# The expert layers' up-projection with coefficients as the stationary operand, and part of VectorE's splitting and one-hot work on GpSimd

## The chip, the cores and the metric

The kernel runs on one core of one Trainium2 chip, in one launch. The metric is the device time in microseconds (us). The kernel before has been run three times: 2917.88 us in the median, 2916.68 to 2918.5 us. TensorE (PE) multiplies matrices: one operand, 128 x 128 here, is loaded into the array and stays (the stationary operand, a weight load), the other is streamed through it column by column (the moving operand), and the products are added up in PSUM, the accumulators' memory. VectorE (DVE), ScalarE (ACT) and GpSimd (POOL) work elementwise, and SyncE (SP) starts the transfers. SBUF is the on-chip memory of 128 partitions.

## The reference, cut to what matters

256 tokens of width 1024 run through two layers of a first block (a mixer and an expert layer each) and two layers of a second block (a mixer, cross attention and a gated feed-forward layer each). The change touches the two expert layers alone:

```python
PEER_HEADS, PEER_NKEYS, PEER_TOPK = 8, 128, 16      # 128 * 128 = 16384 experts

def peer_ffn(x, w_query, sub_keys, down, up):
    q = (xt @ w_query).reshape(T, H, 2, PEER_HALF)
    s = jnp.einsum('thcd,cnd->thcn', q, sub_keys)
    sv, si = lax.top_k(s, K)                          # per half of the key
    ...                                               # the 16 best pairs i * 128 + j per head
    idx = jnp.take_along_axis(cand_i, pos, axis=-1)
    gate = jax.nn.softmax(top_s, axis=-1)
    ...
        a = jnp.einsum('thkd,td->thk', down[ib], xb)
        c = gb * jax.nn.gelu(a)
        return jnp.einsum('thk,thkd->td', c, up[ib])
```

Each token uses 8 x 16 = 128 of the 16384 experts.

## The kernel before

**No gather.** The kernel computes all 16384 experts for all 256 tokens and zeroes what a token did not choose. An expert's number is i * 128 + j. A *row* here is one i: 128 experts, a 128 x 1024 tile of `down` and one of `up`, 512 KB each. `dscan(half, dst)` multiplies 64 rows of `down` with the normalized tokens and writes gelu of the result to `ga[half]`, for each row 128 experts x 256 tokens. `build(half, dst)` makes, token by token, the matrix of gates and multiplies `ga` by it; what then lies in `ga` are the coefficients. `uscan(half)` multiplies 64 rows of `up` with the coefficients and adds up all 128 rows in four PSUM banks.

**The split.** For accuracy in fp32r each factor is cut into a high part h and a low part l, and a product is three matmuls, h*h, l*h and h*l (`mm3`, lines 303 to 305). A weight tile comes by DMA into `wr`, `wt` (line 248) casts it on ScalarE to `wh` (L255) and subtracts on VectorE, `wl = wr - wh` (L256). `wr`, `wh` and `wl` have four buffers each. The coefficients are split for two rows at a time by `split` (L293 on ScalarE, L294 on VectorE) into a ring of eight slots, `xh` and `xl`.

**The up-projection.** `row` (line 514) takes each of the eight 128 x 128 pieces of a row of `up` as the stationary operand and streams the coefficients, 256 tokens, as the moving one: 8 x 3 = 24 matmuls of 256 columns for a row. The result stands as width x tokens, as the residual `x` does. `tail` (line 410) computes the last two rows accumulator by accumulator and adds each to `x` at once (L425), so that the next stage's first matmuls find their input while the last are running.

**Build.** For a block of 8 tokens VectorE makes two one-hot matrices, `oj` (128 x 1024, fp16) and `oi` (128 x 512), by comparing with a ramp (both L1314), and `gi`, the products of `oi` with the two halves of the gates (L1329, 128 x 1024 fp16). TensorE multiplies them (L1338, 16 matmuls of 64 columns), and VectorE multiplies the result in PSUM into `ga` (L1320). There are two sets of `oj`, `oi` and `gi`. A build has 32 blocks; there are two builds a layer. `oj`, `gi` and `oi` appear in the rows as `sq` and `xres`, the tiles in whose room they lie.

**What sets the order.** `wt` calls `tick`, which runs side work (a generator) as long as it has credit: each weight tile adds R1 = 1150 (routing), R2 = 1500 (the first build, beside the second half of `dscan`) or R3 = 1600 (the second build, beside the first half of `uscan`), and a block costs 600 + 900 + 600 = 2100. With H1 = H2 = 0 side work on VectorE stands behind the last split issued. The rest of the order is a list scheduler's; engines run their own queue in order.

Of the kernel before, what the change touches and what calls it, by code (L numbers as in the profile page):

```python
# [23 lines left out]
F32 = mybir.dt.float32  # L24
# [5 lines left out]
OP = mybir.AluOpType  # L30
# [5 lines left out]
T = 256  # L36
# [161 lines left out]
class K:  # L198
    def __init__(self, ctx, tc, ap, ahead):
        self.tc, self.nc, self.ap, self.ctx = tc, tc.nc, ap, ctx  # L200
        nc = self.nc
        self.P = ctx.enter_context(tc.tile_pool(name="keep", bufs=1))
        self.W = ctx.enter_context(tc.tile_pool(name="wts", bufs=1))
        self.S = ctx.enter_context(tc.tile_pool(name="scr", bufs=1))
        self.ps = ctx.enter_context(tc.tile_pool(name="psum", bufs=1, space=PSUM))
        self.dr = ctx.enter_context(tc.tile_pool(name="dram", bufs=1, space=DRAM))
        self.x = self.P.tile([128, 8, T], F32, name="xres", bufs=1)
        self.nw = self.P.tile([128, 13, 8], F32, name="nw")
        self.eps = self.P.tile([128, 1], F32, name="eps")
        nc.vector.memset(self.eps, EPS)  # L210
        nc.scalar.copy(self.eps, self.eps)
        self.got = []
        for d in range(4):
            nc.sync.dma_start(self.x[:, 2 * d:2 * d + 2], ap["x"][:, 2 * d:2 * d + 2])
            if d == 0:
                nc.sync.dma_start(self.nw, ap["nw"])
                for w in ahead[:1]:
                    self.fetch(w)
        for w in ahead[1:]:
            self.fetch(w)  # L220
        self.ones = self.P.tile([128, 128], F32, name="ones")
        nc.vector.memset(self.ones, 1.0)
        self.ident = self.P.tile([128, 128], F32, name="ident")
        self.tb = None
        ps = self.pst("mx")[:, :128]
        for _ in range(WARM):
            nc.tensor.matmul(ps, self.ones, self.ones, start=True, stop=True)
        self.side, self.rate, self.credit = None, 0.0, 0.0
        self.lows, self.hold = [], None
        self.todo, self.sqs = [], []  # L230

    def cap(self, name, rows=128):
        o, w = _COFF[name]
# [14 lines left out]
    def wt(self, src, w=1024):  # L248
        nc = self.nc
        if not self.got:  # L250
            self.fetch(src)
        r = self.got.pop(0)
        h = self.W.tile([128, 1024], F32R, name="wh", bufs=4)
        l = self.W.tile([128, 1024], F32R, name="wl", bufs=4)
        nc.scalar.copy(h[:, :w], r[:, :w])  # L255
        self.lows.append(nc.vector.tensor_sub(l[:, :w], r[:, :w], h[:, :w].bitcast(F32)).ins.name)  # L256
        n = len(nc.cur_bb.bb.instructions)
        self.tick()
        if self.hold is not None and len(self.lows) > self.hold:
            for i in nc.cur_bb.bb.instructions[n:]:  # L260
                if i.engine == mybir.EngineType.DVE:
                    self.tc.add_manual_dep(i, self.lows[-1 - self.hold], mybir.DependencyInfo(
                        mybir.DependencyClass.NoSync, mybir.DependencyReason.DATA), reason="order")
        return h, l
# [145 lines left out]
    def tail(self, accs, rows, wi, scale=None):  # L410
# [27 lines left out]
        ps, rt, r = self.norm_room()  # L438
# [4 lines left out]
        self.rsqrt(rt, ps)  # L443
        self.diag(r, rt)
        self.bcast(r)

    def rows(self, accs, srcs, bhs, bls, end):

# [663 lines left out]
GS = 32768.0  # L1112
# [5 lines left out]
def peer(k, l, nxt):  # L1118
# [4 lines left out]
    with k.tc.tile_pool(name=f"peer_{l}", bufs=1) as p:  # L1123
# [168 lines left out]
                    V.tensor_sub(g3[:, :, 1], gb, g3[:, :, 0])  # L1292

        k.beside(routing(), R1, H1)
        dscan(0, ga[0])

        sets = [[room[:, starts[i]:starts[i + 1]] for i in range(3)],
# [4 lines left out]
        def build(half, dst):  # L1302
# [20 lines left out]
            for b in range(n + 1):  # L1323
                if b < n:
                    oj, oi, gi, ts_ = parts(b)
                    hot(oj, jS[:, ts_], slice(0, 128))
                    yield 600
                    hot(oi, iS[:, ts_], hs)
                    V.tensor_mul(gi.rearrange("p t q (a d) -> p t q a d", d=2),  # L1329
                                 oi.rearrange("p t (a d) -> p t a d", d=2)[:, :, None].to_broadcast([128, TB, 2, HI // 2, 2]),  # L1330
                                 g3[:, ts_, :, None].to_broadcast([128, TB, 2, HI // 2, 2]))
                    yield 900
# [10 lines left out]
        k.beside(build(0, ga[0]), R2, H2)  # L1343
        dscan(1, ga[1])
        k.drain()
        accs = k.rows_begin()
        ring = [k.S.tile([128, 8, T], F32R, name=n, bufs=1) for n in ("xh", "xl")]
        end = []

# [8 lines left out]
        def uscan(half):  # L1358
            for i in range(half * HI, (half + 1) * HI, 2):
                if i % HI == 0:  # L1360
                    coef(i)
                if i % HI + 2 < HI:
                    coef(i + 2)
                if i == 2 * HI - 2:
                    k.tail(accs, [k.wt(ap[f"up{l}"][e]) + tuple(at(e)) for e in (i, i + 1)], nxt, scale=1.0 / GS)
                else:
                    for e in (i, i + 1):
                        k.row(accs, *k.wt(ap[f"up{l}"][e]), *at(e), e == 0, False)

        k.beside(build(1, ga[1]), R3, H2)  # L1370
        uscan(0)
# [4 lines left out]
        k.x = k.P.tile([128, 8, T], F32, name="xres", bufs=1)  # L1376
        nc.sync.dma_start(k.x, xd)
        uscan(1)
        top.close()
    k.dbg("xp", k.x, l)  # L1380

# [383 lines left out]
```

## Time and profile before

| | |
|---|---|
| median of three runs | 2917.88 us (2916.68 to 2918.5) |
| the profiled execution | 2919.18 us, its span 2917.1 us |
| TensorE busy | 2889.8 us, 99% of the span, 25130 matmuls |
| weight loads | 2836.1 us, 97% |
| VectorE busy | 2077.0 us, 71% |
| ScalarE busy | 1457.7 us, 50% |
| GpSimd busy | 0.2 us, 4 instructions |
| DMA | 511.5 MB, 175 GB/s in the mean |

Busy time counts overlapping instructions once. A duration includes the time in which an instruction's last results leave the pipe, so on TensorE and VectorE the next one starts before the row's duration is over; what an instruction costs its engine in a dense stretch is the distance from its start to the next one's start. The layers of the first expert stage lie from about 230 to 1012 us, those of the second from about 1230 to 2010 us.

### The profile page before, as it was taken

What the parts mean: (1) busy time and instruction counts of PE and PEld (TensorE: products, weight loads), DVE (VectorE), ACT (ScalarE), POOL (GpSimd) and SP (SyncE); (2) the same over time, 40 slices, a digit from 0 to 9 for tenths busy, and PEclk for the clock granted to TensorE, in tenths of its full rate; (3) what the DMA queues carried; (4) which work ended last, traced back from release to release, by engine and by line L of the source; (5) the groups of instructions that cost most, each with busy time, mean ns of one, the idle gap of its engine ahead of it and who ended that gap; (6) DMA issues with size and microseconds to landing.
All of it is one profiled execution on the core that took longest, in us unless ns stands there. A gap on an engine that the chain in (4) does not pass through costs nothing.

```text
span 2917.1 us, 59823 instructions
## 1 busy us (share of the span) xinstructions
PE 2889.8 (99%) x25130; PEld 2836.1 (97%) x25130; DVE 2077.0 (71%) x3484; ACT 1457.7 (50%) x1963; POOL 0.2 (0%) x4
## 2 busy tenths in 40 slices
PE   9999999999999999999999999999999999999998
PEld 8989999999999989999999999999999999999998
DVE  7769978769755586798786895556667656667655
ACT  7655553443444476545434434444546544546544
POOL 0000000000000000000000000000000000000000
PEclk9999999999999999999999999999999999999999
DMA  6655554554555555555545445555455555455553
GB/s 202 182 171 168 182 179 163 166 171 160 188 181 184 179 171 181 176 178 184 169 163 172 163 160 195 182 184 189 153 173 188 179 183 179 162 186 181 174 182 129
DMA packets 150493, 511.50 MB, mean 175 GB/s; under 512 B 17176, under 2 KB 26520, under 8 KB 149200
## 3 DMA queue, kind: packets, MB, share of 16 engines
q1 hardware_dynamic: 145904, 503.02, 53.2%
q10 hardware_dynamic: 4320, 4.67, 0.5%
q8 instruction: 196, 3.21, 0.5%
q14 instruction: 73, 0.60, 0.1%
HBM read 500.23 MB, written 7.39 MB: 174 GB/s over the span
## 4 chain that ended last, share of the span: by engine, by line
PE 95%; ACT 2%; DMA 1%; DVE 1%; issue 0%; SPq 0%; ACTq 0%; DVEq 0%
PE col L303 18%; PE col L305 18%; PE col L304 18%; PE acc L303 12%; PE acc L304 12%; PE acc L305 12%; PE mx L1338 2%; ACT wh L255 1%; PE mx L1162 1%; DMA wr<-in_w_hi 0%; PE acc L658 0%; PE acc L1402 0%; DVE wl L256 0%; PE mx L341 0%; DMA c_tri<-in_consts 0%
## 5 line engine op out<-in xcount | busy, mean ns | idle before, releaser
L255 ACT CAST wh<-wr 128x1024 fp32r<-128x1024 f32 (+1 forms) x922 | 960.3, 1044 | 1276.0 <-PE col L304 594.5
L256 DVE TENSOR_TENSOR wl<-wr,wh 128x1024 fp32r<-128x1024 f32 (+1 forms) x922 | 1120.4, 1217 | 608.1 <-ACT wh L255 605.4
L303 PE MATMUL col<-xh,wh 128*128 128x256 f32 x3856 | 1104.7, 286 | 2.3 <-ACT silg L1574 0.9
L305 PE MATMUL col<-xh,wl 128*128 128x256 f32 x3856 | 1096.1, 284 | 4.6 <-DVE wl L256 4.6
L304 PE MATMUL col<-xl,wh 128*128 128x256 f32 x3856 | 1094.7, 284 | 0.0
L305 PEld LDWEIGHTS col<-xh,wl 128*128 128x128 f32 x3856 | 741.7, 192 | 6.8 <-DVE wl L256 5.4
L303 PEld LDWEIGHTS col<-xh,wh 128*128 128x128 f32 x3856 | 742.0, 192 | 4.5 <-ACT silg L1574 1.7
L304 PEld LDWEIGHTS col<-xl,wh 128*128 128x128 f32 x3856 | 742.0, 192 | 0.1
L303 PE MATMUL acc<-xh,wh 128*128 128x256 f32 x2016 | 574.4, 285 | 2.1 <-ACT xh L293 2.1
L304 PE MATMUL acc<-xl,wh 128*128 128x256 f32 x2016 | 570.5, 283 | 0.0
L305 PE MATMUL acc<-xh,wl 128*128 128x256 f32 x2016 | 570.1, 283 | 0.0
L303 PEld LDWEIGHTS acc<-xh,wh 128*128 128x128 f32 x2016 | 386.4, 192 | 2.4 <-ACT xh L293 2.4
L304 PEld LDWEIGHTS acc<-xl,wh 128*128 128x128 f32 x2016 | 387.1, 192 | 0.0
L305 PEld LDWEIGHTS acc<-xh,wl 128*128 128x128 f32 x2016 | 386.9, 192 | 0.0
L1320 DVE TENSOR_TENSOR ga<-ga,mx 128x512 f32<-128x512 f32 x128 | 87.3, 685 | 41.5 <-PE mx L1338 39.5
L304 PE MATMUL acc<-fl,wh 128*128 128x256 f32 x352 | 98.1, 279 | 0.0
L305 PE MATMUL acc<-fh,wl 128*128 128x256 f32 x352 | 98.0, 279 | 0.0
L303 PE MATMUL acc<-fh,wh 128*128 128x256 f32 x352 | 97.7, 280 | 0.0
L294 DVE TENSOR_TENSOR xl<-ga,xh 128x512 fp32r<-128x512 f32 x126 | 85.7, 683 | 0.0
L293 ACT CAST xh<-ga 128x512 fp32r<-128x512 f32 x126 | 76.9, 615 | 0.0
L1179 ACT ACTIVATE ga<-col 128x512 f32<-128x512 f32 x128 | 75.7, 592 | 0.0
L303 PE MATMUL col<-wh,xh 128*128 128x512 f32 (+3 forms) x192 | 70.7, 372 | 3.4 <-ACT hg L1076 2.0
(466 smaller groups left out, 3420.0 us busy)
## 6 DMA issues: line engine op xcount, KB each, us to landing
wr<-in_down SPq DMA_DIRECT2D x256, 512.0 KB, 3.5
wr<-in_up SPq DMA_DIRECT2D x256, 512.0 KB, 3.9
wr<-in_w SPq DMA_DIRECT2D x132, 512.0 KB, 3.9
wr<-in_w_in SPq DMA_DIRECT2D x106, 512.0 KB, 4.0
wr<-in_xa_k SPq DMA_DIRECT2D x16, 512.0 KB, 4.0
wr<-in_xa_v SPq DMA_DIRECT2D x16, 512.0 KB, 4.3
wr<-in_w_out SPq DMA_DIRECT2D x16, 512.0 KB, 3.4
wr<-in_w_q SPq DMA_DIRECT2D x16, 512.0 KB, 3.5
```

The lines of the kernel that those rows point to most:

```text
L255: nc.scalar.copy(h[:, :w], r[:, :w])
L256: self.lows.append(nc.vector.tensor_sub(l[:, :w], r[:, :w], h[:, :w].bitcast(F32)).ins.name)
L293: self.nc.scalar.copy(h, src)
L294: self.nc.vector.tensor_sub(l, src, h.bitcast(F32))
L303: mm(ps, ah, bh, start=first, stop=False, skip_group_check=True)
L304: mm(ps, ah, bl, start=False, stop=False, skip_group_check=True)
L305: mm(ps, al, bh, start=False, stop=last, skip_group_check=True)
L1162: nc.tensor.matmul(ps[:, j], qT[:, h + j, tt * 128:(tt + 1) * 128], sk, start=True, stop=True)
L1179: nc.scalar.activation(dst[:, j * T:(j + m) * T], ps[:, :m].rearrange("p a t -> p (a t)"), AF.Gelu_apprx_tanh)
L1320: V.tensor_mul(dv, dv, ps.rearrange("p t i -> p i t"))
L1338: nc.tensor.matmul(ps[:, t], oj[:, t], gi[:, t, q], start=q == 0, stop=q == 1, skip_group_check=True)
```

## The change

- `wt` has a counter: from `dscan(0)` to the end of `uscan(1)` (`k.share = 4`) GpSimd instead of VectorE makes the low part of every fourth weight tile, 64 a layer.
- `gi` is made by GpSimd, 64 instructions a layer.
- The up-projection is turned round: `trow` takes 128 tokens' coefficients as the stationary operand and streams 512 columns of the row of `up`; for a row 4 x 3 = 12 matmuls of 512 columns. Two successive matmuls (h*h and h*l) have the same coefficients. The four PSUM banks now hold tokens x width.
- `ttail` takes the place of `tail` at the layer's end: each accumulator is scaled and copied to SBUF (ScalarE or VectorE), turned back by TensorE in 128 x 128 transposes, 16 in all, and added to `x`.

```diff
--- before.py
+++ after.py
@@ -228,6 +228,7 @@
         self.side, self.rate, self.credit = None, 0.0, 0.0
         self.lows, self.hold = [], None
         self.todo, self.sqs = [], []
+        self.share, self.turn = 0, 0
 
     def cap(self, name, rows=128):
         o, w = _COFF[name]
@@ -253,7 +254,11 @@
         h = self.W.tile([128, 1024], F32R, name="wh", bufs=4)
         l = self.W.tile([128, 1024], F32R, name="wl", bufs=4)
         nc.scalar.copy(h[:, :w], r[:, :w])
-        self.lows.append(nc.vector.tensor_sub(l[:, :w], r[:, :w], h[:, :w].bitcast(F32)).ins.name)
+        self.turn += 1
+        if self.share and self.turn % self.share == 0:
+            nc.gpsimd.tensor_sub(l[:, :w], r[:, :w], h[:, :w].bitcast(F32))
+        else:
+            self.lows.append(nc.vector.tensor_sub(l[:, :w], r[:, :w], h[:, :w].bitcast(F32)).ins.name)
         n = len(nc.cur_bb.bb.instructions)
         self.tick()
         if self.hold is not None and len(self.lows) > self.hold:
@@ -443,6 +448,53 @@
         self.rsqrt(rt, ps)
         self.diag(r, rt)
         self.bcast(r)
+
+    def trow(self, accs, rows, done=None):
+
+
+        mm = self.nc.tensor.matmul
+        for half, tt in ((0, 0), (0, 1), (1, 0), (1, 1)):
+            n = 2 * half + tt
+            ts, ws = slice(tt * 128, tt * 128 + 128), slice(half * 512, half * 512 + 512)
+            for h, l, bh, bl, first, last in rows:
+                mm(accs[n], bh[:, ts], h[:, ws], start=first, stop=False, skip_group_check=True)
+                mm(accs[n], bh[:, ts], l[:, ws], start=False, stop=False, skip_group_check=True)
+                mm(accs[n], bl[:, ts], h[:, ws], start=False, stop=last, skip_group_check=True)
+            if done is not None:
+                done(n)
+
+    def ttail(self, accs, rows, wi, scale, room):
+
+        self.pre(wi)
+        z = [room.tile([128, 512], F32, name="zt", bufs=2) for _ in range(2)]
+
+        def turn(half):
+            for j in range(2):
+                d = 2 * half + j
+                pt = self.pst("mx", [128, 2, T])
+                for c in range(2):
+                    for tt in range(2):
+                        self.nc.tensor.transpose(pt[:, c, tt * 128:(tt + 1) * 128],
+                                                 z[tt][:, (2 * j + c) * 128:(2 * j + c + 1) * 128], self.ident)
+                xs = self.x[:, 2 * d:2 * d + 2]
+                self.nc.vector.tensor_add(xs, pt, xs)
+                if d < 2:
+                    self.squares(xs)
+                self.pre_pair(d)
+
+        def done(n):
+            t = n % 2
+            if n == 2:
+                turn(0)
+                z[:] = [room.tile([128, 512], F32, name="zt", bufs=2) for _ in range(2)]
+            if t:
+                self.nc.vector.tensor_scalar(z[t], accs[n], scale, None, op0=OP.mult)
+            else:
+                self.nc.scalar.mul(z[t], accs[n], scale)
+            if n == 3:
+                turn(1)
+        self.trow(accs, [r + (False, i == len(rows) - 1) for i, r in enumerate(rows)], done)
+        self.todo = self.norm_steps()
 
     def rows(self, accs, srcs, bhs, bls, end):
 
@@ -1292,6 +1344,7 @@
                     V.tensor_sub(g3[:, :, 1], gb, g3[:, :, 0])
 
         k.beside(routing(), R1, H1)
+        k.share, k.turn = 4, 0
         dscan(0, ga[0])
 
         sets = [[room[:, starts[i]:starts[i + 1]] for i in range(3)],
@@ -1326,7 +1379,7 @@
                     hot(oj, jS[:, ts_], slice(0, 128))
                     yield 600
                     hot(oi, iS[:, ts_], hs)
-                    V.tensor_mul(gi.rearrange("p t q (a d) -> p t q a d", d=2),
+                    nc.gpsimd.tensor_mul(gi.rearrange("p t q (a d) -> p t q a d", d=2),
                                  oi.rearrange("p t (a d) -> p t a d", d=2)[:, :, None].to_broadcast([128, TB, 2, HI // 2, 2]),
                                  g3[:, ts_, :, None].to_broadcast([128, TB, 2, HI // 2, 2]))
                     yield 900
@@ -1343,7 +1396,7 @@
         k.beside(build(0, ga[0]), R2, H2)
         dscan(1, ga[1])
         k.drain()
-        accs = k.rows_begin()
+        accs = [k.pst("acc") for _ in range(4)]
         ring = [k.S.tile([128, 8, T], F32R, name=n, bufs=1) for n in ("xh", "xl")]
         end = []
 
@@ -1362,10 +1415,10 @@
                 if i % HI + 2 < HI:
                     coef(i + 2)
                 if i == 2 * HI - 2:
-                    k.tail(accs, [k.wt(ap[f"up{l}"][e]) + tuple(at(e)) for e in (i, i + 1)], nxt, scale=1.0 / GS)
+                    k.ttail(accs, [k.wt(ap[f"up{l}"][e]) + tuple(at(e)) for e in (i, i + 1)], nxt, 1.0 / GS, q)
                 else:
                     for e in (i, i + 1):
-                        k.row(accs, *k.wt(ap[f"up{l}"][e]), *at(e), e == 0, False)
+                        k.trow(accs, [(*k.wt(ap[f"up{l}"][e]), *at(e), e == 0, False)])
 
         k.beside(build(1, ga[1]), R3, H2)
         uscan(0)
@@ -1376,6 +1429,7 @@
         k.x = k.P.tile([128, 8, T], F32, name="xres", bufs=1)
         nc.sync.dma_start(k.x, xd)
         uscan(1)
+        k.share = 0
         top.close()
     k.dbg("xp", k.x, l)
```

**VectorE in the second build of the first layer**, a little over two blocks. L256 (after: L261) is the split, L1314 (L1367) the one-hots, `oi` with 512 and `oj` with 1024 columns, L1320 (L1373) the scaling, L294 (L299) the coefficients' split, L1329 the product `gi`. Before:

```order
L256 TENSOR_TENSOR wl<-wr,wh 128x1024
L1314 TENSOR_TENSOR xres<-io_2291,rstd 128x512
L1320 TENSOR_TENSOR ga_2293<-ga_2293,mx 128x64x8
L1314 TENSOR_TENSOR xres<-io_2291,jS 128x1024
L1329 TENSOR_TENSOR xres<-xres 128x1024
L256 TENSOR_TENSOR wl<-wr,wh 128x1024
L1314 TENSOR_TENSOR xres<-io_2291,rstd 128x512
L294 TENSOR_TENSOR xl<-ga_2297,xh 128x512
L1320 TENSOR_TENSOR ga_2293<-ga_2293,mx 128x64x8
L1314 TENSOR_TENSOR sq<-io_2291,jS 128x1024
L1329 TENSOR_TENSOR sq<-xres 128x1024
```

The same engine in the same stretch, after:

```order
L261 TENSOR_TENSOR wl<-wr,wh 128x1024
L1367 TENSOR_TENSOR xres<-io_2291,rstd 128x512
L299 TENSOR_TENSOR xl<-ga_2297,xh 128x512
L1373 TENSOR_TENSOR ga_2293<-ga_2293,mx 128x64x8
L1367 TENSOR_TENSOR sq<-io_2291,jS 128x1024
L1367 TENSOR_TENSOR xres<-io_2291,rstd 128x512
L1373 TENSOR_TENSOR ga_2293<-ga_2293,mx 128x64x8
L1367 TENSOR_TENSOR xres<-io_2291,jS 128x1024
L261 TENSOR_TENSOR wl<-wr,wh 128x1024
L299 TENSOR_TENSOR xl<-ga_2297,xh 128x512
```

The product `gi` is gone from VectorE's queue, and between the fifth row and the ninth a split is missing. An `oi` now waits until GpSimd has read the `oi` of two blocks earlier.

**GpSimd in the same stretch, after** (before, its queue is empty there). L259 is the split of a weight tile, L1382 the product `gi`:

```order
L259 TENSOR_TENSOR wl<-wr,wh 128x1024
L1382 TENSOR_TENSOR sq<-xres 128x1024
L1382 TENSOR_TENSOR xres<-xres 128x1024
L1382 TENSOR_TENSOR sq<-xres 128x1024
L259 TENSOR_TENSOR wl<-wr,wh 128x1024
L1382 TENSOR_TENSOR xres<-xres 128x1024
L1382 TENSOR_TENSOR sq<-xres 128x1024
L1382 TENSOR_TENSOR xres<-xres 128x1024
L259 TENSOR_TENSOR wl<-wr,wh 128x1024
```

Three products (at some places two) stand between two splits. A product waits for VectorE's `oi` and for TensorE's matmuls of two blocks earlier; a split waits for ScalarE's cast, and the split behind a waiting product waits with it.

**TensorE at the end of the first layer's up-projection, after** (before, the 24 matmuls of each of the last two rows are followed directly by L303 of the next stage). L460 to L462 are the up-projection, L477 the transposes, L308 to L310 the next stage's first matmuls:

```order
L460 MATMUL acc<-wh,ch 128x512
L461 MATMUL acc<-wl,ch 128x512
L462 MATMUL acc<-wh,cl 128x512
L477 MATMUL mx<-ident,zt 128x128 x2
L308 MATMUL col<-xh,wh 128x256
L477 MATMUL mx<-ident,zt 128x128 x6
L309 MATMUL col<-xl,wh 128x256
L310 MATMUL col<-xh,wl 128x256
```

Eight transposes stand ahead of the last six matmuls of the up-projection, and the eight of the second half behind them, with the next stage's first matmul among them; these last eight wait for the copies of the third and the fourth accumulator.

## Rows read from the trace of the kernel before

**Rows 1.** The page: busy time of each engine, and TensorE's granted clock in 40 slices.
```profile
PE 2889.8 (99%) x25130; PEld 2836.1 (97%) x25130; DVE 2077.0 (71%) x3484; ACT 1457.7 (50%) x1963; POOL 0.2 (0%) x4
...
PEclk9999999999999999999999999999999999999999
```

**Rows 2.** Waits of TensorE over the whole span: in total, times, longest, in us.
```profile
PE col L305 <- DVE wl L256: 4.6, 4, 2.3
```

**Rows 3.** Windows, builds and `uscan(1)`: span; PE, PEld, DVE, ACT, POOL busy us; PEclk, DMA, GB/s.
```profile
429.20:566.70 137.50, 137.50 (x1490) 136.25 (x1488) 114.90 (x160) 54.46 (x63) 0.00 (x0) 1.00 0.50 161
642.60:761.20 118.60, 118.60 (x1298) 117.45 (x1296) 110.93 (x161) 47.10 (x54) 0.00 (x0) 1.00 0.50 159
800.00:980.00 180.00, 180.00 (x1502) 180.00 (x1501) 95.78 (x95) 82.91 (x96) 0.00 (x0) 1.00 0.57 184
```

**Rows 4.** Timeline of TensorE, matmuls of 256 columns in `uscan(1)`: start and duration, us.
```profile
899.76 0.28 PE L303 MATMUL acc<-xh,wh 128*128 128x256 f32 x1
...
903.00 0.28 PE L303 MATMUL acc<-xh,wh 128*128 128x256 f32 x1
```

**Rows 5.** Timeline of TensorE, matmuls of 512 columns, tokens stationary, second block.
```profile
2082.94 0.39 PE L303 MATMUL col<-wh,xh 128*128 128x512 f32 x1
...
2088.16 0.39 PE L305 MATMUL col<-wh,xl 128*128 128x512 f32 x1
```

**Rows 6.** The same form in the first mixer.
```profile
179.06 0.40 PE L303 MATMUL col<-wh,memh 128*128 128x512 f32 x1
...
182.79 0.40 PE L304 MATMUL col<-wl,memh 128*128 128x512 f32 x1
```

**Rows 7.** Timeline of VectorE, one block of the second build: start and duration, us.
```profile
668.01 1.22 DVE L256 TENSOR_TENSOR wl<-wr,wh 128x1024 fp32r<-128x1024 f32 x1
669.15 0.42 DVE L1314 TENSOR_TENSOR xres<-io,rstd 128x512 f16<-128x512 f16 x1
669.48 0.69 DVE L294 TENSOR_TENSOR xl<-ga,xh 128x512 fp32r<-128x512 f32 x1
670.09 0.68 DVE L1320 TENSOR_TENSOR ga<-ga,mx 128x512 f32<-128x512 f32 x1
670.68 0.69 DVE L1314 TENSOR_TENSOR sq<-io,jS 128x1024 f16<-128x1024 f16 x1
671.29 0.69 DVE L1329 TENSOR_TENSOR sq<-xres 128x1024 f16<-128x1024 f16 x1
```

**Rows 8.** Timeline of TensorE: first matmuls of a block at both ends of both builds.
```profile
429.18 0.29 PE L1338 MATMUL mx<-xres 128*128 128x64 f16 x4
...
566.74 0.23 PE L1338 MATMUL mx<-xres 128*128 128x64 f16 x2
...
642.60 0.29 PE L1338 MATMUL mx<-sq 128*128 128x64 f16 x4
...
761.22 0.26 PE L1338 MATMUL mx<-xres 128*128 128x64 f16 x3
```

**Rows 9.** GpSimd's instructions in the whole trace, grouped (one of four such rows).
```profile
L1754 POOL MEMSET const-bfloat16-1.0<- 128x1 bf16 x1 | 0.1, 102 | 0.0
```

**Rows 10.** Timeline of ScalarE and VectorE in `uscan(1)`: the cast and the split of one tile.
```profile
1001.36 1.05 ACT L255 CAST wh<-wr 128x1024 fp32r<-128x1024 f32 x1 [1.83 <-PE acc L304]
...
1002.44 1.23 DVE L256 TENSOR_TENSOR wl<-wr,wh 128x1024 fp32r<-128x1024 f32 x1 [1.66 <-ACT wh L255]
```

**Rows 11.** The layer's end: TensorE's timeline, VectorE's timeline, TensorE's transposes elsewhere.
```profile
1012.58 0.28 PE L305 MATMUL acc<-ch,wl 128*128 128x256 f32 x1
1012.70 0.29 PE L303 MATMUL col<-xh,wh 128*128 128x256 f32 x1
...
1011.93 0.68 DVE L425 SCALAR_TENSOR_TENSOR xres<-acc,xres 128x512 f32<-128x512 f32 x1
...
2091.57 0.82 PE L1444 MATMUL mx<-ident,roc 128*128 128x128 f32 x6
2092.14 0.36 PE L304 MATMUL col<-xl,wh 128*128 128x256 f32 x1
```

## The prediction

> **What bounds the kernel now.** I read the busy times first, then TensorE's waits, then the stretches that the change touches, then distances between starts. TensorE is busy for 99% of the span at a granted clock of 0.9 or more in all 40 slices [rows 1], and over the whole span its longest item of waiting, for VectorE's splits, is 4.6 us in total [rows 2]. So the time is the number of matmuls times the distance between their starts, and work taken from another engine gains nothing by itself. In the windows of the two builds TensorE has no idle time at its upper level of 2.4 GHz (granted 1.00), GpSimd has nothing at all, and VectorE is busy for 114.9 of 137.5 us and for 110.9 of 118.6 us [rows 3]: in the second build 94%, so VectorE is a close second there. In `uscan(1)`, without side work, it is at 53%.
>
> **The turned matmuls.** Between 899.76 and 903.00 us lie 27 distances between starts of 256-column matmuls, 0.120 us each [rows 4]; a row's 24 take 2.88 us. The form that takes their place is in the trace: 512 columns of weights streamed, 128 tokens stationary, in the same order of three (two successive matmuls with the same stationary operand). From 2082.94 to 2088.16 us there are 23 distances, 0.227 us each [rows 5]; in the first mixer 16 distances from 179.06 to 182.79 us give 0.233 us [rows 6]. A row becomes 12 x 0.227 = 2.72 us, or 2.80 us. I take the former, since its operands (`wh`, `wl`, `xh`, `xl`) are the change's own. That is 0.156 us a row (bound 0.08), for all 256 rows 40 us (bound 21 us) if TensorE stays the bound. Holding the coefficients for two matmuls brings nothing of its own: in those rows each of the three follows at the same distance.
>
> **The end of a layer.** Before, the next stage's first matmul follows the last of the up-projection after 0.12 us [rows 11]. Afterwards 16 transposes a layer are added; six took 0.57 us elsewhere [rows 11], so 1.5 us. The last eight wait for the copy of the fourth accumulator, for which I take the 0.68 us of VectorE's 128x512 pass over PSUM [rows 11], with two hand-offs; and the next stage's first matmuls wait for an addition, a square and a scaling behind the first transposes. Before, all that ran beside the remaining matmuls. I put the wait at 2 us (0 to 5). Both layers: 2 x 3.5 = 7 us lost (3 to 13).
>
> **What leaves VectorE.** A block costs 2100 credits; a weight tile gives 1500 in the first build and 1600 in the second, so a block spans 1.40 and 1.31 tiles. Starts of blocks agree: 30 blocks from 429.18 to 566.74 us are 4.59 us each, 27 from 642.60 to 761.22 us 4.39 us [rows 8]. Distances between VectorE's starts: split 1.14, `oi` 0.33, coefficients' split 0.61, scaling 0.59, `oj` 0.61 [rows 7]; `gi` has the form of `oj`, also 0.61. The change takes 0.61 (`gi`) and a quarter of the splits off it, 0.40 or 0.37 us: 1.0 us a block. What remains with two SBUF operands is, in the first build, 0.61 + 0.33 + 1.40 x 0.75 x 1.14 = 2.14 us; in the second, with half a coefficients' split a tile, 0.61 + 0.33 + 1.31 x (0.75 x 1.14 + 0.5 x 0.61) = 2.46 us. The scaling (0.59) reads one of its operands from PSUM.
>
> **What it puts on GpSimd.** The trace has no such operation there, only memsets of one column [rows 9]. From below I bound an operation of 128x1024 with two operands by VectorE's price for the split, 1.14 us; from above I have no row, and work with three times that, 3.4 us. I take twice, 2.3 us, for both kinds, the middle. A block then costs GpSimd 2.3 + 1.40/4 x 2.3 = 3.1 us, or 2.3 + 1.31/4 x 2.3 = 3.05 us. The Trainium skill, GPSIMD Engine Reference, "Performance versus the Vector engine", gives a measured tensor_tensor of 2048 fp32 columns as 4497 ns against VectorE's 2293; half of it, 2.25 us as an estimate, would leave the sum where it is, and no run here shows it yet.
>
> Is one late product a stall? A cast starts as TensorE leaves a tile, the tile's split ends 2.3 us later [rows 10], and TensorE has three other tiles first, 8.6 us: a lead of over 6 us, and a block's products have two sets. So a single operation of 2.3 us, or the load that GpSimd's first use may bring, is hidden. Only throughput counts. By itself 3.1 us fits into a block of 4.2 to 4.6 us.
>
> **In turn or side by side.** What no row shows is whether a GpSimd operation with two SBUF operands and a VectorE operation with two run at once. If none of it overlaps, a block needs 2.14 + 3.1 = 5.24 us in the first build (4.59 before) and 2.46 + 3.05 = 5.51 us in the second (4.39 before), and TensorE waits for the products and splits. For TensorE to stay fed in the second build, where it would need 4.39 - 1.31 x 0.156 = 4.19 us, 43% of GpSimd's time would have to lie beside VectorE's; to come out even in all, about a quarter. My judgement, since no row decides, is that they take turns: 1.0 us comes off VectorE and 3 us go on GpSimd, and for a gain both the price and the overlap must come out well, while VectorE had 6% to spare.
>
> The Trainium skill, SBUF — State Buffer, "Who interferes with whom", says that a VectorE instruction with two SBUF inputs contends with a GpSimd instruction that reads SBUF, and that the second to start is blocked until the first is done. By that the sum is the forecast's; without it, the first rival's. No row of before can show it.
>
> **The sum.** First builds: 0.65 x 32 blocks = 21 us. Second: 1.12 x 28 = 31 us (the first four blocks fall into the change from one scan to the next). Per layer 52, both 104 us. Rows of `up` beside no build: 128 - 28 x 1.31 = 91 a layer, 182 x 0.156 = 28 us gained. Layer ends 7 us. Routing and the scans' remainders: VectorE loses every fourth split, GpSimd's 2.3 us come once in four tiles (11.5 us), nothing. 104 - 28 + 7 = +83 us on the profiled execution's 2919.2 us (span 2917.1), which is 1.3 us above the median: **forecast 3001 us**.
>
> **The rivals.**
> *Side by side* (the other side): GpSimd's work runs beside VectorE's, TensorE stays the bound, and the change gives -40 + 7 = -33 us, 2885 us; at 0.233 us a matmul -14 us, 2904 us. For it: VectorE then has 2.46 + 0.59 = 3.05 us in a block of 4.2, more room than now. It decides from an overlap of about a quarter, or from a GpSimd price under 1.7 us even in turn (2.46 + 1.33 x 1.7 = 4.7 us a block, whose loss the 28 us repay). Against: both are required of an engine that the trace doesn't show working.
> *About even*: partial overlap or a price near 1.7 us, with the gain in the unloaded rows paid back in the builds: 2912 to 2924 us.
> *GpSimd alone too slow*: at 3.4 us an operation it needs 4.5 us a block by itself, and in turn with VectorE about 7 us: 2.1 x 32 + 2.6 x 28 = 140 us a layer, 2918 + 280 - 21 = 3177 us. Side by side it would be near 2905. I hold it unlikely.
>
> **How the numbers follow.** In turn 0.50 (own range 2935 to 3070, by the same sum for prices from 1.9 to 2.7 us), side by side 0.38, about even 0.08, too slow 0.04. 0.2% (6 us) is about what a measurement of this kernel can tell from no change. So faster by more than that 0.38, within it 0.08 (the even case), slower 0.54. Both signs hold much, so the range reaches from the side-by-side end to the in-turn end: 2884 to 3080 us, with some 0.12 left out.
>
> **What would show it.** Turned matmuls 0.227 us apart in `uscan(1)` (right) or 0.24 (no gain). GpSimd's starts in a dense stretch 2.3 us apart. In the builds: blocks 5.2 and 5.5 us apart, TensorE idle in front of L1391 with GpSimd as the releaser, and VectorE's split or one-hot stretched far beyond 1.2 and 0.7 us while GpSimd works, would show turns; blocks of 4.5 and 4.2 us and unstretched rows would show the first rival. At the layer's end, an idle time of some 2 us ahead of L477 or L308. I am wrong if VectorE's rows keep their lengths beside GpSimd's.

## The result and the profile after

The changed kernel takes **2964.95 us** (median of four runs, 2962.62 to 2968.34), against 2917.28 us (2915.08 to 2918.5) before: a ratio of 1.0165, with a 95% interval from 1.0148 to 1.0183. It is 47.7 us slower; the forecast was 83 us slower. The profiled execution took 2965.96 us, with a span of 2964.2 us against 2917.1.

The page of the changed kernel, busy times and the shares of the chain that ended last (before: [rows 1]):

```profile
PE 2877.6 (97%) x22090; PEld 2680.9 (90%) x22090; DVE 2147.4 (72%) x3232; ACT 1460.2 (49%) x1967; POOL 608.0 (21%) x260
...
PE 80%; DVE 14%; issue 3%; ACT 2%; DMA 1%; ACTq 0%; SPq 0%; DVEq 0%
```

252 instructions fewer run on VectorE [rows 1], and yet it is busy for 70 us more, and it holds 14% of the chain. Its windows of the first build, the second build and `uscan(1)` (columns as in [rows 3]; the stretches follow the blocks, so they begin and end elsewhere):

```profile
426.30:571.10 144.80, 139.68 (x1491) 136.49 (x1490) 144.14 (x119) 54.48 (x63) 91.24 (x40) 1.00 0.44 150
651.30:795.60 144.30, 124.17 (x893) 97.51 (x892) 143.81 (x128) 48.75 (x56) 87.69 (x38) 0.96 0.39 129
830.00:1000.00 170.00, 170.00 (x751) 140.90 (x751) 82.15 (x80) 82.67 (x95) 36.63 (x16) 1.00 0.60 193
```

In both builds VectorE is now busy all the time, 144.14 of 144.80 us and 143.81 of 144.30, and TensorE is idle for 5 and 20 us; without a build TensorE is busy throughout. The bound has changed engines, and only in the builds. TensorE's timeline at both ends of both builds, the first matmuls of a block (answers to [rows 8]):

```profile
426.28 0.64 PE L1391 MATMUL mx<-xres 128*128 128x64 f16 x16
...
571.08 0.64 PE L1391 MATMUL mx<-xres 128*128 128x64 f16 x16
...
651.33 0.64 PE L1391 MATMUL mx<-xres 128*128 128x64 f16 x16
...
795.64 0.64 PE L1391 MATMUL mx<-xres 128*128 128x64 f16 x16
```

30 distances of 4.83 us, and 28 of 5.15 us, against 4.59 and 4.39 before. What a block does, on VectorE and GpSimd, stands in their common timeline (the second build; start, duration in us):

```profile
664.35 0.41 DVE L1367 TENSOR_TENSOR xres<-io,rstd 128x512 f16<-128x512 f16 x1
664.69 0.67 DVE L1373 TENSOR_TENSOR ga<-ga,mx 128x512 f32<-128x512 f32 x1
664.91 1.91 POOL L1382 TENSOR_TENSOR sq<-xres 128x1024 f16<-128x1024 f16 x1 [1.56 <-DVE xres L1367]
665.28 2.08 DVE L1367 TENSOR_TENSOR xres<-io,jS 128x1024 f16<-128x1024 f16 x1
666.77 2.84 POOL L259 TENSOR_TENSOR wl<-wr,wh 128x1024 fp32r<-128x1024 f32 x1
667.28 3.41 DVE L261 TENSOR_TENSOR wl<-wr,wh 128x1024 fp32r<-128x1024 f32 x1
```

The one-hot `oj` at 665.28 takes 2.08 us instead of 0.69 [rows 7]: the product on GpSimd ends at 666.82, and what is left of `oj`'s time after that, 0.54 us, is a little less than its usual length. The split at 667.28 takes 3.41 us instead of 1.22; GpSimd's split ends at 669.61, and 1.08 us are left. And GpSimd's split, whose row begins at 666.77, takes 2.84 us, against 2.41 in the median (row in the experiments). The scaling at 664.69, which reads one operand from PSUM, keeps its 0.67 us.

TensorE's waits over the whole span (in total, times, longest, in us; before: [rows 2]):

```profile
PE mx L1391 <- DVE xres L1367: 23.8, 15, 3.1
PE mx L1391 <- DVE sq L1367: 19.9, 11, 3.1
PE acc L462 <- DVE xl L299: 11.0, 2, 5.5
...
PE mx L1391 <- POOL sq L1382: 1.6, 2, 0.8
```

TensorE waits in front of the one-hot matmuls, as forecast, but for VectorE's `oj`, held up behind GpSimd; for GpSimd's own product it waits 1.6 us in all.

### The profile page after: what moved, and what is told of

Its sections match the earlier page's. It is cut to its first block, busy times and chain, and to the rows that moved or that the text cites. A ratio compares the mean times of both kernels' runs of the same rounds, so it can differ in the third digit from the quotient of the medians.

```text
span 2964.2 us, 54006 instructions
## 1 busy us (share of the span) xinstructions
PE 2877.6 (97%) x22090; PEld 2680.9 (90%) x22090; DVE 2147.4 (72%) x3232; ACT 1460.2 (49%) x1967; POOL 608.0 (21%) x260
## 3 DMA queue, kind: packets, MB, share of 16 engines
q8 instruction: 173, 2.83, 0.4%
## 4 chain that ended last, share of the span: by engine, by line
PE 80%; DVE 14%; issue 3%; ACT 2%; DMA 1%; ACTq 0%; SPq 0%; DVEq 0%
PE col L308 16%; PE col L310 16%; PE col L309 16%; PE acc L462 6%; PE acc L460 6%; PE acc L461 6%; DVE xres L1367 4%; DVE wl L261 4%; PE acc L308 3%; PE acc L309 3%; PE acc L310 3%; DVE sq L1367 2%; DVE ga L1373 2%; DVE xl L299 1%; PE mx L1391 1%
## 5 line engine op out<-in xcount | busy, mean ns | idle before, releaser
L256 ACT CAST wh<-wr 128x1024 fp32r<-128x1024 f32 (+1 forms) x922 | 960.4, 1045 | 1104.5 <-PE col L309 562.0
L261 DVE TENSOR_TENSOR wl<-wr,wh 128x1024 fp32r<-128x1024 f32 (+1 forms) x794 | 1039.6, 1313 | 566.1 <-ACT wh L256 562.9
L308 PE MATMUL col<-xh,wh 128*128 128x256 f32 x3856 | 1105.8, 287 | 2.0 <-ACT silg L1628 0.8
L310 PE MATMUL col<-xh,wl 128*128 128x256 f32 x3856 | 1097.9, 285 | 5.6 <-DVE wl L261 5.6
L310 PEld LDWEIGHTS col<-xh,wl 128*128 128x128 f32 x3856 | 742.9, 193 | 8.8 <-DVE wl L261 7.2
L308 PEld LDWEIGHTS col<-xh,wh 128*128 128x128 f32 x3856 | 743.0, 193 | 4.6 <-ACT silg L1628 1.7
L259 POOL TENSOR_TENSOR wl<-wr,wh 128x1024 fp32r<-128x1024 f32 x128 | 331.4, 2589 | 1195.7 <-ACT wh L256 1195.7
L462 PE MATMUL acc<-wh,xl 128*128 128x512 f32 x1008 | 397.8, 395 | 11.0 <-DVE xl L299 11.0
L460 PE MATMUL acc<-wh,xh 128*128 128x512 f32 x1008 | 403.4, 400 | 0.4 <-ACT xh L298 0.4
L461 PE MATMUL acc<-wl,xh 128*128 128x512 f32 x1008 | 397.7, 395 | 2.7 <-DVE wl L261 2.3
L462 PEld LDWEIGHTS acc<-wh,xl 128*128 128x128 f32 x1008 | 192.5, 191 | 52.9 <-DVE xl L299 11.9
L461 PEld LDWEIGHTS acc<-wl,xh 128*128 128x128 f32 x1008 | 192.4, 191 | 43.2 <-DVE wl L261 4.6
L460 PEld LDWEIGHTS acc<-wh,xh 128*128 128x128 f32 x1008 | 192.4, 191 | 38.9 <-ACT xh L298 0.6
L1382 POOL TENSOR_TENSOR xres<-xres 128x1024 f16<-128x1024 f16 x64 | 138.3, 2161 | 153.2 <-PE mx L1391 78.2
L1382 POOL TENSOR_TENSOR sq<-xres 128x1024 f16<-128x1024 f16 x64 | 140.1, 2189 | 92.0 <-DVE xres L1367 44.9
L299 DVE TENSOR_TENSOR xl<-ga,xh 128x512 fp32r<-128x512 f32 x126 | 95.1, 758 | 67.2 <-ACT xh L298 67.2
L1367 DVE TENSOR_TENSOR xres<-io,rstd 128x512 f16<-128x512 f16 x128 | 115.2, 904 | 0.0
L1367 DVE TENSOR_TENSOR xres<-io,jS 128x1024 f16<-128x1024 f16 x64 | 112.3, 1755 | 0.0
L1367 DVE TENSOR_TENSOR sq<-io,jS 128x1024 f16<-128x1024 f16 x64 | 105.0, 1641 | 0.0
```

The costliest lines, as they stand in the source:

```text
L259: nc.gpsimd.tensor_sub(l[:, :w], r[:, :w], h[:, :w].bitcast(F32))
L299: self.nc.vector.tensor_sub(l, src, h.bitcast(F32))
L308: mm(ps, ah, bh, start=first, stop=False, skip_group_check=True)
L310: mm(ps, al, bh, start=False, stop=last, skip_group_check=True)
L460: mm(accs[n], bh[:, ts], h[:, ws], start=first, stop=False, skip_group_check=True)
L461: mm(accs[n], bh[:, ts], l[:, ws], start=False, stop=False, skip_group_check=True)
```

## The experiments

Three theories had to be told apart. *Turns*: a VectorE operation and a GpSimd operation that both read two operands from SBUF run one after the other, and in the builds their sum is the bound. *Late operand*: TensorE waits because GpSimd delivers later. *Turned*: the new form of the up-projection itself makes the stalls.

**The turned form alone.** GpSimd gets nothing:

```diff
-        k.share, k.turn = 4, 0
...
-                    nc.gpsimd.tensor_mul(gi.rearrange("p t q (a d) -> p t q a d", d=2),
+                    V.tensor_mul(gi.rearrange("p t q (a d) -> p t q a d", d=2),
```

> The turned up-projection alone; the products and all weight splits are back on VectorE. Theory 'turns' (VectorE's and GpSimd's operations with two SBUF operands take turns, and that is the whole loss): TensorE is the bound again, 256 rows x 0.156 us = 40 us gained, 5 us lost at the two layer ends, 2917 - 35 = 2882 us (2876 to 2895); blocks of the first build 4.4 us apart (1.40 x 24 x ... of 2.72 + 0.17 us of products), of the second 4.2 us; VectorE's one-hots back at about 0.4 and 0.7 us. Rival 'turned' (the new form of the up-projection, whose matmuls need VectorE's splits sooner, makes the stalls): 2917 us or more, and TensorE still waits for VectorE in the second build.

Measured: **2881.19 us** (2876.86 to 2886.48), a ratio of 0.9868 (0.9847 to 0.9888). Its windows of the first and the second build:

```profile
430.50:568.20 137.70, 137.70 (x1500) 136.41 (x1499) 115.03 (x161) 54.61 (x64) 0.00 (x0) 1.00 0.50 162
641.10:760.30 119.20, 119.20 (x914) 95.17 (x913) 115.04 (x168) 48.30 (x55) 0.00 (x0) 1.00 0.52 168
```

TensorE has no idle time in either. *Turned* falls, and this half of the change is a gain of 36 us. Blocks of the second build are 4.24 us apart. Those of the first stay at 4.59, since it lies beside the down-projection, which isn't turned (the 4.4 us of the expectation overlooked that).

**GpSimd's two pieces alone.** The up-projection is that of before:

```diff
-        accs = [k.pst("acc") for _ in range(4)]
+        accs = k.rows_begin()
...
-                    k.ttail(accs, [k.wt(ap[f"up{l}"][e]) + tuple(at(e)) for e in (i, i + 1)], nxt, 1.0 / GS, q)
+                    k.tail(accs, [k.wt(ap[f"up{l}"][e]) + tuple(at(e)) for e in (i, i + 1)], nxt, scale=1.0 / GS)
...
-                        k.trow(accs, [(*k.wt(ap[f"up{l}"][e]), *at(e), e == 0, False)])
+                        k.row(accs, *k.wt(ap[f"up{l}"][e]), *at(e), e == 0, False)
```

> GpSimd's two pieces alone; the up-projection is as before (256 columns a matmul, no transposes). 'Turns': VectorE and GpSimd together set the length of a block, whatever TensorE does, so blocks are again 4.8 and 5.15 us apart as in the changed kernel; (4.83 - 4.59) x 32 + (5.15 - 4.39) x 28 + 6 us at the change of scans = 35 us a layer, 2917 + 70 = 2987 us (2975 to 3000). 'Turned': near 2917 us (to 2925), blocks 4.6 and 4.4 us apart.

Measured: **2993.32 us** (2987.63 to 2994.98), a ratio of 1.0256 (1.0239 to 1.0273). The whole loss, and more than that of the changed kernel, is GpSimd's. Blocks are 4.78 and 5.11 us apart, nearly as in the changed kernel, though TensorE has the matmuls of before.

**One piece at a time.** The turned form with the splits alone on GpSimd (the products as in the first experiment), and with the products alone (without the line `k.share, k.turn = 4, 0`):

> The turned up-projection with every fourth weight split on GpSimd, the products on VectorE. 'Turns': in the second build a block needs VectorE's 0.61 + 0.33 + 0.61 + 1.31 x (0.75 x 1.14 + 0.5 x 0.61) = 3.1 us, GpSimd's 0.33 x 2.84 = 0.93 us and the scaling's 0.59 us, 4.6 us in all against TensorE's 4.2 (4.0 if the scaling lies beside GpSimd): 2882 + 2 x 28 x (0 to 0.4) = 2882 to 2905 us, I say 2897. Rival 'late operand' (what costs is that TensorE waits for results that come later from GpSimd, not the turns): a late split has a lead of 6 us, so nothing is lost and this equals the turned form alone, within 3 us; VectorE's splits keep 1.2 us.

> The turned up-projection with the products of one-hots and gates on GpSimd, all weight splits on VectorE. 'Turns': in the second build 0.61 + 0.33 + 1.31 x (1.14 + 0.5 x 0.61) = 2.83 us of VectorE's two-operand work plus 1.9 us on GpSimd, 4.73 us a block (5.3 if the scaling doesn't overlap) against TensorE's 4.2; in the first 0.61 + 0.33 + 1.40 x 1.14 + 1.9 = 4.44 us against 4.4: about 17 us a layer and 3 us at the change of scans, 2882 + 40 = 2922 us (2910 to 2945). 'Late operand': all of the loss is here, 2960 us or more, with TensorE's one-hot matmuls waiting for GpSimd's products and VectorE's rows at their old lengths.

Measured: splits alone **2892.59 us** (2888.3 to 2896.8), a ratio of 0.9914 (0.9897 to 0.993); products alone **2918.6 us** (2915.55 to 2924.66), 1.0005 (0.9995 to 1.0014). VectorE's one-hot `oj` in every second block of the second build (min/median/max in ns, first and last start), in three kernels. The turned form alone:

```profile
L1366 DVE TENSOR_TENSOR xres<-io,jS x14: 681/686/687, 641.1 to 749.4; 128x1024 f16<-128x1024 f16 x14
```

With the splits on GpSimd:

```profile
L1367 DVE TENSOR_TENSOR xres<-io,jS x14: 683/684/2734, 643.2 to 753.4; 128x1024 f16<-128x1024 f16 x14
```

With the products on GpSimd:

```profile
L1366 DVE TENSOR_TENSOR xres<-io,jS x14: 675/1794/2079, 641.8 to 768.3; 128x1024 f16<-128x1024 f16 x14
```

The same instruction, 0.68 us long by itself, is stretched to as much as 2.7 us beside a split and to some 1.8 to 2.1 us beside a product. With the splits alone it is stretched only now and then; blocks stay 4.24 us apart, and TensorE stays the bound. Of its 11 us over the turned form alone the two profiled executions show 4, and these lie at the change from scan to scan, where TensorE waits 1.5 us for a coefficients' split in each layer; the rest I can't place. The pieces don't add: 37 and 11 us over the turned form, but 84 together. The first piece uses up VectorE's spare time, and the second then counts in full.

GpSimd's own prices in the changed kernel (min/median/max in ns; all splits, and every second product of the second build):

```profile
L259 POOL TENSOR_TENSOR wl<-wr,wh x128: 2390/2408/3427, 227.7 to 2046.7; 128x1024 fp32r<-128x1024 f32 x128
```

```profile
L1382 POOL TENSOR_TENSOR xres<-xres x14: 1902/2219/2756, 652.1 to 786.0; 128x1024 f16<-128x1024 f16 x14
```

**Work that nobody waits for.** To part *turns* from *late operand* for good, three kernels leave the turned form alone as it is and let GpSimd, in the second builds, write into a dead part of `ga0`: the block's product once more, a copy of the one-hots (one operand), or two memsets behind a copy of four columns.

```diff
+                    if half:
+                        dum = ga[0][:, 0:512].bitcast(F16).rearrange("p (t q a d) -> p t q a d", t=TB, q=2, d=2)
+                        src = oi.rearrange("p t (a d) -> p t a d", d=2)[:, :, None].to_broadcast([128, TB, 2, HI // 2, 2])
+                        nc.gpsimd.tensor_mul(dum, src, g3[:, ts_, :, None].to_broadcast([128, TB, 2, HI // 2, 2]))
```

In the second kernel the last line is `nc.gpsimd.tensor_copy(dum, src)`, in the third

```diff
+                        nc.gpsimd.tensor_copy(dum[:, 0:1, 0:1, 0:2], src[:, 0:1, 0:1, 0:2])
+                        nc.gpsimd.memset(dum, 0.0)
+                        nc.gpsimd.memset(dum, 0.0)
```

> The turned form alone, with nothing taken from VectorE; in the second build of each layer GpSimd makes each block's product of one-hots and gates once more, into a buffer that nobody reads. 'Turns': 3.44 us of VectorE's two-operand work in a block (2.83 with the product's 0.61) plus 1.9 us of GpSimd's, 5.3 us a block instead of 4.2; 31 intervals x 1.1 = 34 us and about 4 us at the change of scans, per layer: 2881 + 76 = 2957 us (2940 to 2975), VectorE's one-hots of 0.69 us at up to 2.1 us. 'Late operand' (the loss is TensorE waiting for what GpSimd makes): nobody waits for this product, so 2881 us as in the turned form alone, VectorE's rows unstretched.

> As the run with idle products, but GpSimd copies the one-hots (one SBUF operand, same 128x1024 output). The duration of such a copy is in no trace yet. If a reading GpSimd takes its turn with VectorE whatever the number of its operands, a block is 3.44 us plus the copy's duration where that is above 4.2, and some of VectorE's two-operand rows end with the copy, longer than 0.69 us by up to its duration; at a copy of 1.3 us that is 4.7 us a block, 2881 + 2 x 31 x 0.5 = 2912 us. If it takes two operands on both engines, VectorE's rows stay at 0.42, 0.69 and 1.22 us and the time at 2881 us (2876 to 2887). I expect turns, at a smaller price than the product's: 2890 to 2930 us.

> As the run with idle products, but GpSimd copies four columns of the one-hots (so that it keeps the blocks' pace) and then sets the 128x1024 buffer twice, without reading it. If what matters is that GpSimd reads SBUF, VectorE's rows keep 0.42, 0.69 and 1.22 us but for the tiny copy's share, blocks stay 4.2 us apart, 2881 us (2876 to 2890). If any work of GpSimd on SBUF stops VectorE, a block is 3.44 us plus both sets, and the rows of VectorE stretch to their length.

Measured: products **2955.65 us** (2948.71 to 2958.08), a ratio of 1.0134 (1.0117 to 1.0151); copies **2894.88 us** (2892.71 to 2897.18), 0.9922 (0.9905 to 0.9938); memsets **2882.37 us** (2880.73 to 2886.98), 0.9881 (0.9865 to 0.9898). A product that no instruction reads costs 74 us, and in its trace no engine has a wait for GpSimd, VectorE included, whose `oi` may be overwritten only once that product has read it: *late operand* falls. Timeline of the kernel with idle products, VectorE and GpSimd:

```profile
681.53 1.21 DVE L261 TENSOR_TENSOR wl<-wr,wh 128x1024 fp32r<-128x1024 f32 x1
681.74 4.83 POOL L1387 TENSOR_TENSOR ga<-xres 128x1024 f16<-128x1024 f16 x1 [4.57 <-DVE xres L1366]
...
682.66 0.67 DVE L299 TENSOR_TENSOR xl<-ga,xh 128x512 fp32r<-128x512 f32 x1
683.27 1.21 DVE L261 TENSOR_TENSOR wl<-wr,wh 128x1024 fp32r<-128x1024 f32 x1
684.40 0.41 DVE L1366 TENSOR_TENSOR xres<-io,rstd 128x512 f16<-128x512 f16 x1
684.74 0.67 DVE L1372 TENSOR_TENSOR ga<-ga,mx 128x512 f32<-128x512 f32 x1
685.34 1.79 DVE L1366 TENSOR_TENSOR xres<-io,jS 128x1024 f16<-128x1024 f16 x1
```

Here both sides of a turn can be seen. I read GpSimd's row of 4.83 us as 1.9 us of work (its shortest rows) behind 2.9 us in which VectorE runs four operations of two SBUF operands at their usual lengths; it ends at 686.57, 1.83 us after VectorE came to the scaling with its PSUM operand (684.74). Then `oj`, due at 685.34, lasts 1.79 us, to half a microsecond beyond that end. With copies:

```profile
678.87 0.68 DVE L299 TENSOR_TENSOR xl<-ga,xh 128x512 fp32r<-128x512 f32 x1
679.08 1.37 POOL L1387 COPY ga<-xres 128x1024 f16<-128x1024 f16 x1 [2.15 <-DVE xres L1366]
679.47 0.68 DVE L1372 TENSOR_TENSOR ga<-ga,mx 128x512 f32<-128x512 f32 x1
680.07 0.92 DVE L1366 TENSOR_TENSOR sq<-io,jS 128x1024 f16<-128x1024 f16 x1
```

The copy takes turns too, with one operand. It is shorter (1.04 us at the least), gets in at the scaling, and most of it is over when `oj` begins: 0.92 us instead of 0.68. With memsets:

```profile
683.08 0.68 DVE L1372 TENSOR_TENSOR ga<-ga,mx 128x512 f32<-128x512 f32 x1
683.27 0.95 POOL L1388 MEMSET ga<- 128x1024 f16 x1
683.68 0.68 DVE L1366 TENSOR_TENSOR sq<-io,jS 128x1024 f16<-128x1024 f16 x1
684.28 0.95 POOL L1389 MEMSET ga<- 128x1024 f16 x1
684.28 0.68 DVE L1381 TENSOR_TENSOR sq<-xres 128x1024 f16<-128x1024 f16 x1
```

Nothing is stretched: in the whole second build of the first layer the one-hots `oj` stay at 0.69 us or less. So it is neither GpSimd's load nor its writing, but its reading of SBUF. The Trainium skill, SBUF — State Buffer, "Who interferes with whom", says just this: two SBUF inputs on VectorE contend with a GpSimd instruction that reads SBUF, not with one that only writes, and a VectorE instruction with at most one SBUF input, outside its 2-port modes, doesn't contend. These rows agree: the product and the copy, which read, stretch `oj` to 1.79 and 0.92 us, the memset leaves it at 0.68, and the scaling, with one SBUF input, keeps its 0.67 us beside the product.

**Turns, in numbers.** If the two engines take turns, a block in a build needs VectorE's work with two SBUF operands plus GpSimd's reading work, unless TensorE needs longer. With the prediction's rows for VectorE and, for GpSimd, the shortest durations of product and copy (1.90 and 1.04 us) and the median of the split (2.41 us):

| kernel, build | VectorE + GpSimd, us | TensorE, us | measured block, us |
|---|---|---|---|
| changed, first | 2.14 + 1.90 + 0.35 x 2.41 = 4.88 | 4.59 | 4.83 |
| changed, second | 2.46 + 1.90 + 0.33 x 2.41 = 5.16 | 4.24 | 5.15 |
| GpSimd alone, first | 2.14 + 1.90 + 0.35 x 2.41 = 4.88 | 4.59 | 4.78 |
| GpSimd alone, second | 2.46 + 1.90 + 0.33 x 2.41 = 5.16 | 4.39 | 5.11 |
| turned, products | 2.83 + 1.90 = 4.73 | 4.24 | 4.71 |
| turned, splits | 3.07 + 0.33 x 2.41 = 3.87 | 4.24 | 4.24 |
| idle products | 3.44 + 1.90 = 5.34 | 4.24 | 5.45 |
| idle copies | 3.44 + 1.04 = 4.48 | 4.24 | 4.44 |
| idle memsets | 3.44 | 4.24 | 4.24 |

The lower five are second builds; a measured block is the distance between the first and the last start of a block's one-hot matmuls, divided by the number of blocks between (27 or 28, in a first build 30). The larger of the two sides agrees with each to about 0.1 us.

**Coefficients not held.** The turned form alone, with the coefficients' low half second instead of third:

```diff
-                mm(accs[n], bh[:, ts], l[:, ws], start=False, stop=False, skip_group_check=True)
-                mm(accs[n], bl[:, ts], h[:, ws], start=False, stop=last, skip_group_check=True)
+                mm(accs[n], bl[:, ts], h[:, ws], start=False, stop=False, skip_group_check=True)
+                mm(accs[n], bh[:, ts], l[:, ws], start=False, stop=last, skip_group_check=True)
```

> The turned form alone, with the three matmuls of a group in another order, so that no two successive ones share their coefficients: the low half of the coefficients comes second, not third. If holding the coefficients brings nothing of its own (the prediction's step), 512-column matmuls stay 0.227 us apart and the time is that of the turned form, 2881 us (2876 to 2887). If every third matmul went faster for keeping its stationary operand, this order would be slower by more than that: at the 0.233 us that some 512-column rows of the first mixer show, 0.08 us a row and 20 us in all, 2901 us.

Measured: **2878.91 us** (2875.82 to 2882.24), a ratio of 0.9868 (0.9852 to 0.9884), that of the turned form. Holding brings nothing: the page of the changed kernel lists as many weight loads (22090) as matmuls. So the gain lies in the 512-column form itself.

The turned form alone, in either order, beats both kernels: 36 us faster than before, 84 us faster than the changed kernel.

## Why the prediction was right, and where its sizes were off

The direction and the mechanism were right: in turn, with VectorE and GpSimd together as the bound in the builds. That they take turns was a judgement with a chance of 0.50, which no row of before could decide. The range held the time; the forecast lay 36 us too high. Term by term, for both layers (measured between the same blocks of the two kernels, by the starts of their first matmuls; first plus second layer):

| term | forecast, us | measured, us |
|---|---|---|
| first builds, first to last block | +42 | 7.2 + 6.0 = +13.3 |
| second builds, fourth to last block | +62 | 22.4 + 21.5 = +43.9 |
| change from scan to scan, first to fourth block of the second build | 0 | 7.7 + 7.9 = +15.6 |
| `up` rows beside no build | -28 | -13.5 - 13.5 = -27.0 |
| layer ends | +7 | 2 x 2.3 = +4.6 |
| sum | +83 | +50.4 (the spans: +47.1) |

The stretches outside these terms were 3 us shorter in the changed kernel's execution. That the forecast lay no further off is partly luck: the builds came out 47 us cheaper than forecast, and the change from scan to scan, left out, gave 16 us of that back.

*GpSimd's price.* This is the step that failed in size. I took 2.3 us for both kinds; the split is 2.41, but the product, of which each block has one, 1.90. With the measured prices the forecast's own formula gives 4.88 and 5.16 us instead of 5.24 and 5.51, and the builds cost 62 us in place of 104, where 57 were measured. The price came from between two bounds far apart (1.14 and 3.4 us), and no row could narrow it. The Trainium skill's GPSIMD Engine Reference, "Performance versus the Vector engine", led to an estimate of 2.25 us for the fp32 split, 7% below the 2.41 of these rows; for the fp16 product it has no figure, and using one price for both kinds was my choice.

*The change from scan to scan.* The forecast leaves these blocks out, which puts them at nothing without a reason. Before, the second build's first block begins at 625.36 us (TensorE's timeline, the row below) and its fourth at 642.60 [rows 8], 17.2 us later; in the changed kernel at 629.70 and 654.66, 25.0 us.

```profile
625.36 0.64 PE L1338 MATMUL mx<-xres 128*128 128x64 f16 x16
```

TensorE's timeline of the changed kernel there:

```profile
629.70 0.64 PE L1391 MATMUL mx<-xres 128*128 128x64 f16 x16
...
639.10 1.65 PE L462 MATMUL acc<-wh,xl 128*128 128x512 f32 x3 [5.52 <-DVE xl L299]
640.54 0.63 PE L460 MATMUL acc<-wh,xh 128*128 128x512 f32 x1
...
644.38 0.49 PE L460 MATMUL acc<-wh,xh 128*128 128x512 f32 x1
...
654.66 0.64 PE L1391 MATMUL mx<-sq 128*128 128x64 f16 x16
```

The first row of `up` needs the coefficients' low half, and VectorE reaches that split late; its waits ahead of L462 are the 11.0 us of the changed kernel's waits, 5.5 in each layer. Turns are behind this too: ahead of that split stand two `oj` beside a product and a split of GpSimd, which end at 633.43 and 636.19 us. VectorE's timeline:

```profile
631.60 2.39 DVE L1367 TENSOR_TENSOR xres<-io,jS 128x1024 f16<-128x1024 f16 x1
633.91 2.82 DVE L1367 TENSOR_TENSOR sq<-io,jS 128x1024 f16<-128x1024 f16 x1
```

Of the rest of the 7.7 us, 1.8 us are matmuls that run slower behind the wait (last section). I had judged single late operands by their lead and found 6 us; at the start of a scan there is no lead.

*The turned matmuls.* Right: in `uscan(1)` they are 0.227 us apart. TensorE's timeline, 14 distances in 3.17 us:

```profile
899.63 0.39 PE L461 MATMUL acc<-wl,xh 128*128 128x512 f32 x1
...
902.80 0.39 PE L460 MATMUL acc<-wh,xh 128*128 128x512 f32 x1
```

That makes 12 x 0.227 = 2.72 us a row, the forecast's price.

*The layer's end.* Forecast 3.5 us a layer, measured 2.3. TensorE's timeline:

```profile
1032.12 1.03 PE L477 MATMUL mx<-ident,zt 128*128 128x128 f32 x8
1032.91 0.48 PE L460 MATMUL acc<-wh,ch 128*128 128x512 f32 x1
...
1034.39 0.38 PE L477 MATMUL mx<-ident,zt 128*128 128x128 f32 x2
1034.70 0.39 PE L308 MATMUL col<-xh,wh 128*128 128x256 f32 x1
1035.38 0.88 PE L477 MATMUL mx<-ident,zt 128*128 128x128 f32 x6 [0.28 <-DVE zt L491]
1036.01 0.36 PE L309 MATMUL col<-xl,wh 128*128 128x256 f32 x1
```

The first eight transposes take 0.79 us. The second eight lie between 1034.39 and 1036.01 us, together with one matmul of the next stage that would have taken 0.12: 1.5 us. The wait for the copy of the fourth accumulator shows as 0.28 us, not 2.

*The signs to look for.* VectorE's rows stretched as announced, and TensorE is idle ahead of the one-hot matmuls. The releaser I named, GpSimd, was wrong: it is VectorE's `oj`. Whoever looks only for waits on GpSimd sees 1.6 us and misses the cause.

*The first rival*, side by side at 2885 us, had the turned form's price right: alone it takes 2881 us. What did not come was the overlap.

## What to carry to other kernels

Before work goes from VectorE to GpSimd, count in each stretch VectorE's operations with two SBUF operands and add GpSimd's reading work in full: if the sum exceeds what the bounding engine needs, the move is a loss, even where GpSimd alone and VectorE alone would both have room. Work that only writes on GpSimd, or work on VectorE with one operand from SBUF and one from PSUM, stayed out of that sum here. Where a change joins two edits, cost each by itself: here one was worth 36 us, and the other took 84.

## What the runs showed of the hardware

- A turn is not given evenly. In the kernel with idle products, GpSimd's product waited 2.9 us behind four VectorE operations in a row with two SBUF operands, and ran once VectorE came to one with a PSUM operand; VectorE then waited for GpSimd's end. In the changed kernel, GpSimd's split at 666.77 us got in between two such operations, `oj` and VectorE's split. So GpSimd's busy time holds its own waits (608 us in the changed kernel; 64 + 64 products at 1.90 and 128 splits at 2.41 are 552 us), and VectorE's does too.
- A GpSimd copy with one SBUF operand stops VectorE as a product does, for its shorter time. A memset of 128x1024 fp16 took 0.95 us all 128 times and stopped nothing.
- TensorE's wait at the change between the scans cost more than its own length. After the 5.52 us the 512-column matmuls are 0.43 us apart, from 640.54 us on, instead of 0.227, and the granted clock from 639 to 645 us is 0.54 (near the lower level, 1.2 GHz); from 645 us it is 1.00 again (windows below, columns as above). The nine distances up to 644.38 us take 3.84 us instead of 2.04. The turned form alone has 1.00 throughout there; so do the kernels with the splits alone and with the products alone, where the wait at the same place is 1.5 and 2.1 us.

```profile
639.00:645.00 6.00, 5.90 (x15) 4.71 (x16) 3.67 (x6) 1.04 (x1) 0.00 (x0) 0.54 0.00 0
645.00:651.00 6.00, 6.00 (x28) 4.95 (x27) 3.36 (x4) 2.63 (x3) 0.00 (x0) 1.00 0.44 154
```
